# A score scale with its minimum in one VectorE operation, and inverse roots by Newton steps, in a two-layer hybrid attention step

## The chip, the cores and the metric

The kernel runs on one core of one Trainium2 chip. The metric is the time of one execution on the device in microseconds (us), as the median of several runs. The engines are TensorE (PE, its weight loads PEld), VectorE (DVE), ScalarE (ACT), GpSimd (POOL) and SyncE (SP), which here issues nearly all transfers.

## The reference, cut to what matters

Two layers run over 512 latent tokens (four tiles of 128 rows) and 128 context tokens (one tile, here called the prompt). Each layer norms its input, projects it to all branches at once, runs two attentions and a Fourier branch, gates them, projects back and adds to the input. The change touches the softmax of the two attentions and the norms of queries and keys.

```python
def rms_norm(x, g):
    xf = x.astype(jnp.float32)
    y = xf * lax.rsqrt(jnp.mean(xf * xf, axis=-1, keepdims=True) + RMS_EPS)
    return (y * g.astype(jnp.float32)).astype(x.dtype)

def gqa_attention(q, k, v):
    ...
        sc = jnp.einsum('bqhgd,bkhd->bhgqk', qb, k).astype(jnp.float32) * scale
        pr = jax.nn.softmax(sc, axis=-1).astype(v.dtype)
        o = jnp.einsum('bhgqk,bkhd->bqhgd', pr, v)

def diff_attention(q1, q2, k1, k2, v, lam):
    ...
        pr = jax.nn.softmax(s1, axis=-1) - lam * jax.nn.softmax(s2, axis=-1)
        return jnp.einsum('bhqk,bkhd->bqhd', pr.astype(v.dtype), v)
```

Attention A has 8 query heads of 64 on 2 key heads; attention B has 4 heads of two components of 32, so 8 score blocks as well. A latent row sees 512 latent and 256 cached keys, 768 in all; a prompt row sees the 128 prompt keys. `rms_norm` is taken per head: 8 values per row for the queries of A and for queries and keys of B, 2 for the keys of A, over five tiles: 40 or 10 elements per partition.

## The kernel before

**How the program is made.** The functions of `hybrid_step` don't issue instructions; each call records an operation with its inputs, outputs, the engines that may do it and a price per engine (`Engine.cost`, line 451). `Plan.order` (line 187) then simulates the engines with these prices, chooses for each operation the engine and the place in its queue, and for each tile its buffer, and the result is issued in that order. The engines run their queues strictly in it; semaphores do the rest. So a price, a due time (an operation's number plus a shift from the table `SHIFT`) or a constant of `CFG` changes the order of the whole program. `dag`, `dg`, `da` stand for operations that several engines may do (DVE/ACT/POOL, DVE/POOL, DVE/ACT); `dv`, `ac`, `gp`, `pe`, `sp` name one.

**The stages of a layer.** The projections of the five tiles, each in three fp32r products of a high and a low part (whi, wlo from `load_chunk`), come first, with the Fourier branch between them. Then follows attention B, woven with the projections of A, then attention A, woven with the output projection (ohi, olo from `load_wout`, products with mA, mB, mC).

**Queries and keys.** `squares` sums the squares of a head into a tile MS; when all five tiles are there, `rstds` takes the inverse roots with `rstd_of` (line 597): an addition of 1e-6, then one POOL power with exponent -0.5, into a tile rs. Then the rows are scaled by it, staged as fp16 (st), transposed by a transfer (kTB, qTB, kTA, qTA), and scores can begin.

**One unit of attention** (`unit`, line 1217) is one score block of 128 queries by 768 keys; on the prompt it is four heads of 128 by 128. It runs through these steps:

- PE: the score products into a tile S in two PSUM banks (called banks in the profile); at most three S find room.
- DVE: the row maximum m, a reduction over S.
- ACT or DVE: the bias nb = m times minus the scale plus 13 ln 2 (line 1232), on one element per row (four on the prompt).
- ACT: the exponential in place in PSUM, with that bias and the scale KS as operands, and its row sum into Z. So S holds the exponentials times 2 to the 13.
- ACT (or DVE): the cast of S to fp16, the high half of the tile phl.
- DVE: S less that cast, the low half of phl. Then S is free.
- SP: one transposing transfer of phl to pT.
- PE (`unit_back`, line 1246): 18 small products of pT with V, the split values.

The buffers phl (PHL) and pT (PT) are three each. `normed` later multiplies by VI, the value scale from `split_v` (line 996), over Z.

```python
red(m, S.rearrange("p (i k) -> p i k", i=n), ALU.max)
nb = SM([P, n], "nb")
(da if CFG["nb"] else dv).affine(nb, m, KS[a][:, 2:3], shift13)
```

In the profile, line 427 is the call that issues most operations; lines 434, 437, 440 and 443 are the forms of `affine` and `tensor_copy` on ACT, DVE, POOL and ACT. So the tiles tell the operations apart, not the lines.

Of the kernel before, what the change touches and what calls it, by code (L numbers as in the profile page):

```python
# [31 lines left out]
NH = 8  # L32
EPS = 1e-6
GRID_W = 64
LN_SHIFT = 13.0 * math.log(2.0)

C_QA, C_KA, C_VA, C_GA = 0, 512, 640, 768
C_QB, C_KB, C_VB, C_GB, C_UC, C_GC = 1280, 1536, 1792, 2048, 2304, 2560
# [367 lines left out]
class Engine:  # L406
# [43 lines left out]
    @staticmethod  # L450
    def cost(name, op, outs, ins, k, psum):
        o = outs[0]
        n = max([_free(o)] + [_free(x) for x in ins[:1]])
        if op == "dma_start":
            return (450.0 if name == "SP" else 1000.0), max(90.0, _free(o) * o.ap[0][1] * 4 / 360.0)
        if op == "dma_start_transpose":
            return Plan.TURN, _free(o) * 1.0
        if name == "PE":
            m = _free(o)
            if op == "transpose":  # L460
                return 109.0, 0.0
            dt = k["rhs"].dtype
            if dt == F32:
                return (27.0 if o.offset // Plan.row(o) else max(m / 0.6, 213.0)), 0.0
            return (m / 2.4 + 2.4 if dt == F16 else max(m * 0.457 + 1.0, 107.0)), 0.0
        if name == "ACT":
            return ((70.0 if psum else 93.0) + 0.833 * n + 93.0 * (len(ins) - 1)
                    + (112.0 if k.get("accum_out") is not None else 0.0)), 0.0
        if name == "POOL":
            if k.get("op") == ALU.pow:  # L470
                return 200.0 + 60.0 * n, 0.0
            if op == "tensor_tensor":
                still = any(x.ap[-1][0] == 0 for x in ins)
                return 148.0 + (1.67 if still else 1.95 if F16 in (o.dtype, ins[0].dtype) else 2.19) * n, 0.0
            if op == "memset":
                return 100.0 + 0.5 * n, 0.0
            return 161.0 + (0.833 if k.get("op1") is not None or op in ("tensor_copy", "affine") else 3.4) * n, 0.0
        if op == "reciprocal":
            return 65.0 + 8.3 * n, 0.0
        aps = 2 if op == "affine" else sum(isinstance(k.get(q), bass.AP) for q in ("scalar1", "scalar2", "scalar"))  # L480
        fast = op in ("tensor_copy", "tensor_scalar", "affine") and not psum
        return max(130.0, (98.0 if psum and op != "tensor_reduce" else 68.0) + 60.0 * aps + (0.52 if fast else 1.04) * n), 0.0

# [2 lines left out]
def hybrid_step(ctx: ExitStack, tc: tile.TileContext, x_prompt, x_sample, cache_a, cache_b, c, c_ctx,  # L486
# [60 lines left out]
    def ts(eng, out, a, s1, op0, s2=None, op1=None):  # L547
        if op1 is None:
            return eng.tensor_scalar(out=out, in0=a, scalar1=s1, scalar2=None, op0=op0)
        return eng.tensor_scalar(out=out, in0=a, scalar1=s1, scalar2=s2, op0=op0, op1=op1)  # L550
# [29 lines left out]
    pe.transpose(cols_ps, rows, ident[:32, :32])  # L580
    cols = const.tile([P, 32], F32, name="cols")
    dv.tensor_copy(cols, cols_ps)
    shift13 = const.tile([P, 1], F32, name="shift13")
    gp.memset(shift13, LN_SHIFT)
    mhalf = const.tile([P, 1], F32, name="mhalf")
    gp.memset(mhalf, -0.5)
    zero = const.tile([P, 384], F16, name="zero")
# [8 lines left out]

    def rstd_of(out, ms):

        ts(dg, out, ms, EPS, ALU.add)
        y = mk(mhalf, 0, [[0, d[1]] for d in out.ap[1:]])  # L600
        tt(gp, out, out, y, ALU.pow)
# [192 lines left out]
    for l in range(DEPTH):  # L794
# [200 lines left out]
        @moved("scale")  # L995
        def split_v(a):


            n, h0 = (2, 0) if a else (4, 2)
            mx = SM([P, 3], "vm")  # L1000
            parts = []
            for x, i0, m in kv("v", a):
                parts += [(x, 0, min(m, NKEY - i0), i0)] + ([(x, m - 1, m, i0)] if i0 + m > NKEY else [])
            for j, (x, a0, a1, _) in enumerate(parts):
                dv.tensor_reduce(out=mx[:, j:j + 1], in_=x[:, a0:a1], op=ALU.max, axis=AX.XY, apply_absolute_value=True)
            j0 = len(parts) - 2
# [209 lines left out]
        @moved("front")  # L1216
        def unit(a, t, h, z, o):

            n = 4 if t == PT_ else 1
            w = 4 * P if t == PT_ else NKEY * P  # L1220
            nk = w // P
            S = psS([P, w])
            with plan.together():
                if n == 1:
                    qk(S, a, t, h, 0, w)
                else:
                    for i in range(4):
                        qk(S[:, i * P:(i + 1) * P], a, t, h + i, NKEY * P, (NKEY + 1) * P)
            m = SM([P, n], "m")
            red(m, S.rearrange("p (i k) -> p i k", i=n), ALU.max)  # L1230
            nb = SM([P, n], "nb")
            (da if CFG["nb"] else dv).affine(nb, m, KS[a][:, 2:3], shift13)
            k = w // n
            for i in range(n):
                ac.activation(S[:, i * k:(i + 1) * k], S[:, i * k:(i + 1) * k], AF.Exp,
                              bias=nb[:, i:i + 1], scale=KS[a][:, 1:2],
                              accum_out=z[:, i:i + 1])
            hl = alloc(pool, [P, 2, w], F16, "PHL", "phl")
            da.tensor_copy(hl[:, 0, :], S)
            tt(dv, hl[:, 1, :], S, hl[:, 0, :], ALU.subtract)  # L1240
            pt = alloc(pool, [P, 2 * nk, P], F16, "PT", "pT")
            sp.dma_start_transpose(out=pt, in_=hl.rearrange("p a k -> p (a k)"))
            unit_back(a, t, h, n, nk, pt, o)
# [257 lines left out]
 'late': 0.0,  # L1501
 'keep': {'bank': 0, 'G': 2},
 'ahead': 800,
 'late_dma': 0.0,
 'late_pe': 500.0,
 'dve': 1.8,
 'wait': 300.0,
 'start': ['x0', 'm0', 'x3', 'UC', 'x1', 'x2', 'm2', 'm1', 'm3', 'GC', 'x4', 'm4', 'm5', 'm6', 'm7'],
 'fine': 1,
 'nb': 1,  # L1510
 'tail': 3,
 'early': 3,
 'whole': 0,
# [2 lines left out]
 'spare': [],  # L1516
 'early_0': 1,
 'early_1': 2,
 'tail_1': 3}
SHIFT = {'mix': -100, 'fm': -60, 'norm': 10, 'cached': -25, 'mod': -25, 'out': 25, 'qA': 25, 'finish': 250, 'fo': -25, 'cached0': 10, 'finish1': 100, 'start': -25, 'back0': -100}  # L1520
BUFS = {"G": 16, "H": 14, "T": 5, "T2": 2, "W": 8, "KT": 8, "raw": 2, "P": 3, "PHL": 3, "PT": 3, "ST": 2, "O": 2, "Z": 3,
        "KS": 3, "MS": 5, "gmax": 4, "VS": 3, "sm": 11, "gains": 1}

# [78 lines left out]
```

## Time and profile before

| | us |
|---|---|
| median of 3 runs (810.5 to 819.9) | 812.66 |
| the profiled execution | 810.99 |
| its span from first to last instruction | 808.9 |
| PE busy / idle in the span | 708.9 / 100.0 |
| DVE busy | 546.5 |
| ACT busy | 479.2 |
| POOL busy | 297.2 |

The mean clock granted to TensorE is 0.971 of full speed. The page gives busy shares over the whole span, while the stages have different limits; the windows of the trace show them apart. Projections fill about 40 to 180 us (layer 0) and 440 to 560 us (layer 1); attention and output fill 180 to 440 and 560 to 800 us. A line of a group reads: source line, engine, operation, output tile and inputs, shapes and count, then busy us, mean ns of one, and the idle time ahead with what ended it. Matmul records overlap, so their sum exceeds the engine's busy time. The DMA share is the mean busy share of the 16 transfer engines and can exceed 1 where records overlap.

### The profile page before, as it was taken

The numbers are of one execution on the slowest core, as the hardware profiler recorded it, in microseconds if no ns is written. First come the engines' busy times: TensorE is split into PE (matmuls) and PEld (weight loads), VectorE is DVE, ScalarE is ACT, GpSimd is POOL, SyncE is SP. The second block draws the span as 40 slices with busy tenths as digits, with TensorE's granted clock in tenths as the row PEclk, the third lists the DMA queues.
The fourth block names the chain that finished last, engine by engine and source line by source line (L and its number), as shares of the span: only waits on it lengthen the run. The fifth ranks groups of instructions, "written<-read, shape, count | busy, mean of one in ns | idle before, by whom it ended". The sixth has DMA issues, their size and how long they took to land.

```text
span 808.9 us, 17514 instructions
## 1 busy us (share of the span) xinstructions
PE 708.9 (88%) x6752; PEld 583.9 (72%) x6752; DVE 546.5 (68%) x1062; ACT 479.2 (59%) x969; POOL 297.2 (37%) x308
## 2 busy tenths in 40 slices
PE   4899998999988878878879999988978987988886
PEld 2578897888877855545567999988878876656564
DVE  1564264679799659677686432577998866899674
ACT  4763232478768776565786432246875777688651
POOL 2222005435754425272343101444564343624210
PEclk9999999999999979999989999999999998999899
DMA  8967353898999987999996643298899899799884
GB/s 290 338 196 235 98 171 88 211 179 178 195 160 236 251 182 167 227 258 249 258 173 155 214 132 97 67 171 190 169 184 209 179 218 229 125 167 183 140 162 114
DMA packets 316915, 150.50 MB, mean 186 GB/s; under 512 B 256992, under 2 KB 308048, under 8 KB 316832
## 3 DMA queue, kind: packets, MB, share of 16 engines
q1 hardware_dynamic: 314944, 144.21, 79.8%
q0 software_dynamic: 1888, 5.18, 2.2%
q8 instruction: 53, 0.87, 0.5%
q14 instruction: 30, 0.25, 0.1%
HBM read 77.50 MB, written 8.67 MB: 107 GB/s over the span
## 4 chain that ended last, share of the span: by engine, by line
PE 41%; DMA 31%; DVE 9%; POOL 8%; ACT 5%; issue 4%; SPq 1%; ACTq 0%; DVEq 0%; POOLq 0%
PE banks L427 41%; DMA pT_PT<-phl_PHL 18%; POOL rs_MS L427 5%; DMA raw_raw<-in_w_mod_dram 4%; DMA kTB_KT<-st_ST 3%; DVE phl_PHL L427 3%; DVE m_sm L427 2%; DMA rawo_raw<-in_w_out_dram 2%; DMA raw_raw<-in_w_in_dram 2%; ACT phl_PHL L443 2%; ACT banks L427 1%; SPq L427 1%; DMA x_G<-in_x_sample_dram 1%; POOL qA_H L427 1%; POOL wlo_W L427 1%
## 5 line engine op out<-in xcount | busy, mean ns | idle before, releaser
L427 PE MATMUL banks<-whi_W,hhi_G 128*128 128x256 f32 x880 | 252.4, 290 | 7.3 <-ACT sq_T L427 2.7
L427 PE MATMUL banks<-wlo_W,hhi_G 128*128 128x256 f32 x880 | 252.9, 288 | 0.0
L427 PE MATMUL banks<-whi_W,hlo_G 128*128 128x256 f32 x880 | 252.2, 288 | 0.0
L427 PEld LDWEIGHTS banks<-whi_W,hhi_G 128*128 128x128 f32 x880 | 166.5, 190 | 17.3 <-issue 9.5
L427 PEld LDWEIGHTS banks<-wlo_W,hhi_G 128*128 128x128 f32 x880 | 167.3, 190 | 8.7 <-issue 6.6
L427 PEld LDWEIGHTS banks<-whi_W,hlo_G 128*128 128x128 f32 x880 | 167.2, 190 | 5.4 <-issue 3.3
L427 DVE TENSOR_TENSOR phl_PHL<-banks,phl_PHL 128x768 f16<-128x768 f32 (+1 forms) x136 | 126.1, 935 | 33.6 <-ACT phl_PHL L443 33.0
L427 ACT ACTIVATE banks<-banks,nb_sm,KS_KS 128x768 f32<-128x768 f32 (+1 forms) x160 | 136.8, 855 | 2.5 <-DVE mod L427 0.2
L427 DVE TENSOR_REDUCE m_sm<-banks 128x1 f32<-128x768 f32 (+1 forms) x136 | 125.7, 935 | 18.5 <-PE banks L427 15.6
L427 PE MATMUL banks<-V,pT_PT 128*128 128x64 f16 x2400 | 96.5, 196 | 41.8 <-DMA pT_PT<-phl_PHL 37.9
L427 PEld LDWEIGHTS <-pT_PT 128*128 128x128 f16 x2400 | 82.6, 100 | 68.3 <-DMA pT_PT<-phl_PHL 59.1
L443 ACT ACTIVATE phl_PHL<-banks 128x768 f16<-128x768 f32 (+1 forms) x135 | 106.2, 797 | 34.5 <-DMA pT_PT<-phl_PHL 33.2
L434 ACT ACTIVATE nb_sm<-m_sm,shift,KS_KS 128x1 f32<-128x1 f32 (+1 forms) x106 | 40.4, 383 | 67.0 <-DVE m_sm L427 56.7
L427 PE MATMUL banks<-ohi_W,mA_G 128*128 128x512 f32 x160 | 58.7, 426 | 4.7 <-ACT ohi_W L443 3.2
L427 PE MATMUL banks<-kTA_KT,qTA_H 128*128 128x512 f16 (+2 forms) x288 | 56.9, 332 | 3.7 <-DVE phl_PHL L427 3.4
L427 POOL TENSOR_TENSOR xo_G<-xo_G,go_T 128x512 f32<-128x512 f32 x24 | 31.6, 1320 | 73.1 <-DVE go_T L427 72.9
L427 DVE TENSOR_TENSOR wlo_W<-raw_raw,whi_W 128x1024 fp32r<-128x1024 f32 x33 | 40.3, 1224 | 15.7 <-ACT whi_W L443 8.9
L443 ACT ACTIVATE whi_W<-raw_raw 128x1024 fp32r<-128x1024 f32 x34 | 36.1, 1060 | 19.3 <-DMA raw_raw<-in_w_in_dram 17.3
L427 PEld LDWEIGHTS <-qTA_H 128*128 128x128 f16 x288 | 25.4, 105 | 30.0 <-issue 14.0
L427 POOL TENSOR_TENSOR rs_MS<-rs_MS,mhalf 128x40 f32<-128x40 f32 (+1 forms) x8 | 44.6, 5581 | 0.4
L427 PEld LDWEIGHTS banks<-ohi_W,mA_G 128*128 128x128 f32 x160 | 30.6, 196 | 13.7 <-ACT ohi_W L443 3.9
L427 ACT ACTIVATE sq_T<-banks 128x256 f32<-128x256 f32 (+1 forms) x50 | 17.9, 359 | 37.7 <-PE banks L427 31.6
(257 smaller groups left out, 1147.1 us busy)
## 6 DMA issues: line engine op xcount, KB each, us to landing
raw_raw<-in_w_in_dram SPq DMA_DIRECT2D x44, 512.0 KB, 5.0
raw_raw<-in_w_mod_dram SPq DMA_DIRECT2D x32, 512.0 KB, 4.4
rawo_raw<-in_w_out_dram SPq DMA_DIRECT2D x16, 512.0 KB, 5.1
x<-xo_G SPq DMA_DIRECT2D x10, 512.0 KB, 4.7
xo_G<-x SPq DMA_DIRECT2D x10, 512.0 KB, 5.3
dft_G<-in_dft_s_dram POOLq DMA_DIRECT2D x8, 512.0 KB, 4.3
raw_P<-in_w_mod_dram SPq DMA_DIRECT2D x11, 256.0 KB, 5.5
raw_PHL<-in_w_mod_dram SPq DMA_DIRECT2D x11, 256.0 KB, 5.2
```

The source lines that it names most:

```text
L427: return getattr(real, op)(*[at(x) for x in a], **{q: at(v) for q, v in k.items()})
L434: ways.append((name, dur, dma, lambda real=real: real.activation(at(outs[0]), at(a[1]), AF.Identity, bias=at(a[3]), scale=at(a[2])), None, ...
L443: ways.append((name, dur, dma, lambda real=real: real.activation(at(outs[0]), at(ins[0]), AF.Copy), None, port))
```

## The change

- For a unit of 768 keys, one DVE operation multiplies S in PSUM by minus the scale, writes it back in place, and gives the row minimum as its accumulator m. ACT's exponential takes m as bias with the constant factor -1. The reduction over S and the step nb are gone. On the prompt the reduction stays; a small DVE product gives the bias.
- The factor 2 to the 13 moves from the bias to the cast (now an `affine` with that factor) and to the difference (`scalar_tensor_tensor`); `split_v` divides VI by it.
- `rstd_of` on more than 8 elements (the queries and keys of A and B, eight times in the kernel) is an integer start value and three Newton steps on DVE, eleven instructions in two scratch tiles. Smaller ones keep the POOL power.
- The planner's price of the POOL power rises, its price of a DVE operation counts an accumulator and fewer operands for `affine`, and constants of `CFG` and `SHIFT` are set anew.

```diff
-                return 200.0 + 60.0 * n, 0.0
+                return 440.0 + 158.0 * n, 0.0
...
     def rstd_of(out, ms):
 
+        if _free(out) > 8:
+            v, a = (alloc(pool, [P] + list(out.shape[1:]), F32, "rstd", "r") for _ in range(2))
+            ts(dv, v, ms, EPS, ALU.add)
+            ts(dv, out.bitcast(I32), v.bitcast(I32), -0.5, ALU.mult, 1597463007.0, ALU.add)
+            for _ in range(3):
+                tt(dv, a, out, out, ALU.mult)
+                stt(a, a, -0.5, v, ALU.mult, ALU.mult)
+                stt(out, a, 1.5, out, ALU.add, ALU.mult)
+            return
         ts(dg, out, ms, EPS, ALU.add)
...
             dv.reciprocal(vs, vi)
+            ts(dv, vi, vi, 2.0 ** -13, ALU.mult)
...
             m = SM([P, n], "m")
-            red(m, S.rearrange("p (i k) -> p i k", i=n), ALU.max)
-            nb = SM([P, n], "nb")
-            (da if CFG["nb"] else dv).affine(nb, m, KS[a][:, 2:3], shift13)
             k = w // n
-            for i in range(n):
-                ac.activation(S[:, i * k:(i + 1) * k], S[:, i * k:(i + 1) * k], AF.Exp,
-                              bias=nb[:, i:i + 1], scale=KS[a][:, 1:2],
-                              accum_out=z[:, i:i + 1])
+            if n == 1:
+                dv.tensor_scalar(out=S, in0=S, scalar1=KS[a][:, 2:3], scalar2=3e38, op0=ALU.mult, op1=ALU.min, accum_out=m)
+                ac.activation(S, S, AF.Exp, bias=m, scale=-1.0, accum_out=z)
+            else:
+                red(m, S.rearrange("p (i k) -> p i k", i=n), ALU.max)
+                ts(dv, m, m, KS[a][:, 2:3], ALU.mult)
+                for i in range(n):
+                    ac.activation(S[:, i * k:(i + 1) * k], S[:, i * k:(i + 1) * k], AF.Exp,
+                                  bias=m[:, i:i + 1], scale=KS[a][:, 1:2], accum_out=z[:, i:i + 1])
             hl = alloc(pool, [P, 2, w], F16, "PHL", "phl")
-            da.tensor_copy(hl[:, 0, :], S)
-            tt(dv, hl[:, 1, :], S, hl[:, 0, :], ALU.subtract)
+            da.affine(hl[:, 0, :], S, 2.0 ** 13, 0.0)
+            stt(hl[:, 1, :], S, 2.0 ** 13, hl[:, 0, :], ALU.mult, ALU.subtract)
...
- 'late_dma': 0.0,
- 'late_pe': 500.0,
- 'dve': 1.8,
- 'wait': 300.0,
+ 'late_dma': 500.0,
+ 'late_pe': 650.0,
+ 'dve': 1.9,
+ 'wait': 250.0,
...
- 'tail_1': 3}
+ 'tail_1': 2}
...
+ 'kA1': -170,
+ 'norm1': 50,
```

What the order does with it shows at three places. The first is ACT at the end of attention A in layer 1, before; Z is the row sum, KS the scale, mA the gated output of a tile.

```order
L434 ACTIVATE nb_1931_sm_12274<-m_1930_sm_12267,shift_79,KS_1342_KS_8071 128x1
L427 ACTIVATE mA_1946_G_12278<-banks 128x256
L427 ACTIVATE banks,Z_1883_Z_11999<-banks,nb_1931_sm_12274,KS_1342_KS_8071 128x768
L443 ACTIVATE phl_1932_PHL_12290<-banks 128x768
L434 ACTIVATE nb_1940_sm_12338<-m_1939_sm_12330,shift_79,KS_1342_KS_8071 128x1
```

The same place now:

```order
L433 ACTIVATE phl_1796_PHL_11894<-banks 128x768
L426 ACTIVATE banks,Z_1768_Z_11757<-banks,m_1801_sm_11915 128x768
L433 ACTIVATE phl_1802_PHL_11930<-banks 128x768
L426 ACTIVATE banks,Z_1768_Z_11757<-banks,m_1805_sm_11928 128x768
L433 ACTIVATE phl_1806_PHL_11959<-banks 128x768
```

The nb rows are gone, the exponential reads m itself, and KS is no longer among its operands.

The second place is the inverse root of the keys of B in layer 0. On POOL before (ko is the prompt's keys on their way out, kB the keys):

```order
L427 TENSOR_SCALAR rs_349_MS_3345<-MS_330_MS_3202 128x40
L427 TENSOR_TENSOR rs_349_MS_3345<-rs_349_MS_3345,mhalf 128x40
L427 TENSOR_TENSOR ko_350_T_3398<-kB_275_G_2615,rs_349_MS_3345 128x256
L427 TENSOR_TENSOR kB_274_G_3258<-kB_274_G_3258,rs_349_MS_3345 128x1024
L440 TENSOR_SCALAR st_369_ST_3431<-kB_274_G_3258 128x4x96
```

On DVE now, where r are the scratch tiles and mod the modulation of the next layer:

```order
L426 TENSOR_SCALAR r_349_rstd_3227<-MS_329_MS_3067 128x40
L426 TENSOR_TENSOR t_262_347_T_3230<-banks,tabB_210_H_2543 128x256
L426 TENSOR_SCALAR rs_348_MS_3237<-r_349_rstd_3227 128x40
L426 TENSOR_TENSOR kB_273_G_3137<-kB_273_G_3137,t_262_347_T_3230 128x256
L426 TENSOR_TENSOR r_350_rstd_3242<-rs_348_MS_3237 128x40
L426 SCALAR_TENSOR_TENSOR r_350_rstd_3242<-r_350_rstd_3242,r_349_rstd_3227 128x40
L426 SCALAR_TENSOR_TENSOR rs_348_MS_3237<-r_350_rstd_3242,rs_348_MS_3237 128x40
```

The addition and the power left POOL; the chain stands on DVE among the last evacuations of the keys, two more rounds of three behind the rows shown.

The third place is the end of PE's queue. Before, from the last product with pT (V are the values) on:

```order
L427 MATMUL banks<-V,pT_1942_PT_12378 128x64
L427 MATMUL banks<-olo_1849_W_11797,mA_1946_G_12278 128x512
L427 MATMUL banks<-ohi_1848_W_11766,mA_1946_G_12278 128x512
L427 MATMUL banks<-ident,gA_1599_H_10472 128x128 x2
L427 MATMUL banks<-ohi_1851_W_11871,mA_1946_G_12278 128x512
```

Now:

```order
L426 MATMUL banks<-V,pT_1817_PT_12024 128x64
L426 MATMUL banks<-ohi_1743_W_11494,mA_1819_G_11861 128x512
L426 MATMUL banks<-olo_1744_W_11532,mA_1819_G_11861 128x512
L426 MATMUL banks<-ohi_1743_W_11494,mA_1819_G_11861 128x512
L426 MATMUL banks<-ohi_1746_W_11545,mA_1819_G_11861 128x512
L426 MATMUL banks<-olo_1747_W_11557,mA_1819_G_11861 128x512
L426 MATMUL banks<-ohi_1746_W_11545,mA_1819_G_11861 128x512
L426 MATMUL banks<-ohi_1749_W_11644,mA_1819_G_11861 128x512
L426 MATMUL banks<-olo_1750_W_11657,mA_1819_G_11861 128x512
L426 MATMUL banks<-ohi_1749_W_11644,mA_1819_G_11861 128x512
L426 MATMUL banks<-ident,gA_1519_H_10231 128x128 x2
```

Between the last product with pT and the transposes of the gated rows gA, which wait for it by way of DVE, stood two output products, and now nine of another tile.

More of the change, by code (lines that the diff above doesn't have):

```diff
@@ L34 @@
 GRID_W = 64
-LN_SHIFT = 13.0 * math.log(2.0)
 C_QA, C_KA, C_VA, C_GA = 0, 512, 640, 768
@@ L479, in cost @@
             return 65.0 + 8.3 * n, 0.0
-        aps = 2 if op == "affine" else sum(isinstance(k.get(q), bass.AP) for q in ("scalar1", "scalar2", "scalar"))
+        aps = len(ins) - 1 if op == "affine" else (k.get("accum_out") is not None) + sum(isinstance(k.get(q), bass.AP) for q in ("scalar1", "scalar2", "scalar"))
         fast = op in ("tensor_copy", "tensor_scalar", "affine") and not psum
@@ L582, in hybrid_step @@
     dv.tensor_copy(cols, cols_ps)
-    shift13 = const.tile([P, 1], F32, name="shift13")
-    gp.memset(shift13, LN_SHIFT)
     mhalf = const.tile([P, 1], F32, name="mhalf")
@@ L1503 @@
  'ahead': 800,
- 'late_dma': 0.0,
- 'late_pe': 500.0,
- 'dve': 1.8,
- 'wait': 300.0,
+ 'late_dma': 500.0,
+ 'late_pe': 650.0,
+ 'dve': 1.9,
+ 'wait': 250.0,
  'start': ['x0', 'm0', 'x3', 'UC', 'x1', 'x2', 'm2', 'm1', 'm3', 'GC', 'x4', 'm4', 'm5', 'm6', 'm7'],
  'fine': 1,
- 'nb': 1,
  'tail': 3,
@@ L1518 @@
  'early_1': 2,
- 'tail_1': 3}
-SHIFT = {'mix': -100, 'fm': -60, 'norm': 10, 'cached': -25, 'mod': -25, 'out': 25, 'qA': 25, 'finish': 250, 'fo': -25, 'cached0': 10, 'finish1': 100, 'start': -25, 'back0': -100}
+ 'tail_1': 2}
+SHIFT = {'mix': -100,
+ 'fm': -60,
+ 'norm': 10,
+ 'cached': -25,
+ 'mod': -25,
+ 'out': 25,
+ 'qA': 15,
+ 'finish': 250,
+ 'fo': -25,
+ 'cached0': 10,
+ 'finish1': 100,
+ 'start': -25,
+ 'back0': -100,
+ 'kA1': -170,
+ 'norm1': 50,
+ 'norm0': -10,
+ 'start0': -45,
+ 'back1': -160,
+ 'rows0': 40,
+ 'fab0': -160}
 BUFS = {"G": 16, "H": 14, "T": 5, "T2": 2, "W": 8, "KT": 8, "raw": 2, "P": 3, "PHL": 3, "PT": 3, "ST": 2, "O": 2, "Z": 3,
-        "KS": 3, "MS": 5, "gmax": 4, "VS": 3, "sm": 11, "gains": 1}
+        "KS": 3, "MS": 5, "rstd": 4, "gmax": 4, "VS": 3, "sm": 11, "gains": 1}
 def _split12(x):
```

## The prediction, as it was recorded

> **What bounds the kernel now.** I read the page first: busy shares, then the chain that ended last; then the windows, which put a stage to each share; then the waits of TensorE.
>
> ```profile
> span 808.9 us, 17514 instructions
> PE 708.9 (88%) x6752; PEld 583.9 (72%) x6752; DVE 546.5 (68%) x1062; ACT 479.2 (59%) x969; POOL 297.2 (37%) x308
> PE 41%; DMA 31%; DVE 9%; POOL 8%; ACT 5%; issue 4%; SPq 1%; ACTq 0%; DVEq 0%; POOLq 0%
> PE banks L427 41%; DMA pT_PT<-phl_PHL 18%; POOL rs_MS L427 5%; DMA raw_raw<-in_w_mod_dram 4%; DMA kTB_KT<-st_ST 3%; DVE phl_PHL L427 3%; DVE m_sm L427 2%; DMA rawo_raw<-in_w_out_dram 2%; DMA raw_raw<-in_w_in_dram 2%; ACT phl_PHL L443 2%; AC
> ```
>
> TensorE (PE) is the busiest engine, but the chain spends 31% on transfers, most of it on pT, the transposed probabilities. The reduction m_sm, the POOL power rs_MS and the difference phl_PHL, which the change touches, are on the chain with 2, 5 and 3%.
>
> ```profile
> 120.00:180.00 60.00, 53.72 (x426) 47.98 (x426) 36.74 (x88) 25.16 (x59) 26.48 (x17) 0.94 0.70 160
> 180.00:440.00 260.00, 221.32 (x2317) 174.44 (x2316) 199.14 (x337) 183.31 (x357) 118.66 (x122) 0.96 0.97 206
> 520.00:560.00 40.00, 35.97 (x291) 33.99 (x290) 25.39 (x64) 18.40 (x39) 21.47 (x13) 0.96 0.73 155
> 560.00:800.00 240.00, 208.77 (x2224) 167.08 (x2222) 193.19 (x307) 167.57 (x333) 96.96 (x88) 0.97 0.92 178
> PE banks L427 <- DMA pT_PT<-phl_PHL: 37.9, 38, 2.4
> PE banks L427 <- DVE phl_PHL L427: 10.8, 15, 1.8
> ```
>
> Columns: window, length, PE, PEld, DVE, ACT, POOL, granted clock, DMA share, GB/s. The second and fourth rows are the attention stages of the two layers; the first and third are the ends of the projections ahead of them. In attention PE idles 38.7 and 31.2 us, VectorE (DVE) is busy 77 and 80%, and the DMA engines stand at 0.97 and 0.92: no engine is full but the transfers nearly are. PE's two largest waits are there: 38 times for a transposed block, 15 times for a score bank that the difference has not freed. Ahead of attention PE idles 6.3 and 4.0 us.
>
> **Part 1, the path of one unit (128 units of 768 keys, 8 of the prompt).** The last unit of the kernel, which nothing queues in front of, shows it:
>
> ```profile
> 788.83 0.96 DVE L427 TENSOR_REDUCE m_sm<-banks 128x1 f32<-128x768 f32 x1
> 789.82 0.39 ACT L434 ACTIVATE nb_sm<-m_sm,shift,KS_KS 128x1 f32<-128x1 f32 x1 [4.09 <-DVE m_sm L427]
> 790.24 0.96 ACT L427 ACTIVATE banks<-banks,nb_sm,KS_KS 128x768 f32<-128x768 f32 x1
> 798.28 0.70 PE L427 MATMUL banks<-V,pT_PT 128*128 128x64 f16 x18 [0.95 <-DMA pT_PT<-phl_PHL]
> ```
>
> From the maximum's start to its products takes 9.5 us. The bias step nb_sm costs 0.45 (789.79 to 790.24); a hand-over alone costs 0.03 (789.79 to 789.82). So its removal gives 0.42.
>
> ```profile
> L427 DVE TENSOR_REDUCE m_sm<-banks 128x1 f32<-128x768 f32 x128 | 120.3, 950 | 15.4 <-PE banks L427 12.5 <-ACT phl_PHL L443 1.1 <-POOL rb_sm L427 0.8
> L427 DVE TENSOR_TENSOR phl_PHL<-banks,phl_PHL 128x768 f16<-128x768 f32 x128 | 120.7, 951 | 32.7 <-ACT phl_PHL L443 32.1
> L427 DVE SCALAR_TENSOR_TENSOR V<-vA_G,vs_sm,V 128x768 f16<-128x768 f32 x2 | 2.0, 1008 | 0.0
> L427 ACT ACTIVATION_READ_ACCUMULATOR banks<-banks,nb_sm,KS_KS 128x1 f32 x160 | 31.5, 197 | 0.0
> L427 ACT ACTIVATE banks<-banks,nb_sm,KS_KS 128x768 f32<-128x768 f32 x128 | 123.1, 961 | 2.3 <-DVE mod L427 0.2
> L443 ACT ACTIVATE phl_PHL<-banks 128x768 f16<-128x768 f32 x127 | 101.7, 809 | 33.7 <-DMA pT_PT<-phl_PHL 32.5
> L434 ACT ACTIVATE nb_sm<-m_sm,shift,KS_KS 128x1 f32<-128x1 f32 x98 | 37.3, 383 | 58.8 <-DVE m_sm L427 48.5 <-POOL ob_T L427 7.0 <-POOL xo_G L427 3.1
> L437 DVE TENSOR_SCALAR nb_sm<-m_sm,KS_KS,shift 128x1 f32<-128x1 f32 x30 | 7.9, 267 | 1.1 <-ACT nb_sm L434 0.4
> ```
>
> The scale with minimum takes the reduction's place. No row shows DVE writing PSUM or giving an accumulator. A pass over 768 with a per-partition scalar costs 1.008 (the V row; 0.057 above the difference), which is the low bound; if the minimum has to be read out like ScalarE's sum (the accumulator row, 0.197), 1.205. I take 1.10, between them. VectorE: DVE Perf Modes (the Trainium skill, "Two Vector instructions with no wait between them") says that an op which also writes out its accumulator is two instructions, the main one and an accumulator read; the trace shows such a pair on ACT alone, and by that rule the upper bound holds and the unit's gain below is 0.24. The exponential loses one of two per-partition operands: 961 less 809 (a pass with none) is 152, half of it 0.076. Cast and difference gain a constant factor: nothing for the cast (bounds 0 and +0.076), nothing for the difference (bounds 0 and +0.057). The prompt's eight units keep the reduction and add a 4-element scale of about 0.2 in place of an nb of 0.39: nothing.
>
> Sum per unit: -0.42 + 0.15 - 0.08 = -0.35 (bounds -0.44 and -0.24). ACT loses 37.3 + 3.1 us of nb and 128 x 0.076 = 9.7, which matters little: ACT is 70% busy in attention. DVE gains 128 x 0.15 = 19 and loses 7.9.
>
> What reaches the end is set by PE's 53 waits, 48.7 us. Each shrinks by at most 0.35: 18.6 us. The new order helps too: counted in 256-column matmuls, the weight products that stand on PE between a unit's scores and its pT products rise from 52.6 to 57.0 on average, and in the least covered tenth of the units from 24 to 38. Where nothing but such products run, 175 of them fill 20 us:
>
> ```profile
> 480.00:500.00 20.00, 20.00 (x175) 20.00 (x173) 4.96 (x9) 5.06 (x14) 1.05 (x1) 1.00 0.33 104
> ```
>
> That is 0.114 each, so 0.5 us more cover per unit. Together 0.85 us against a mean wait of 0.92 would take nearly all 48.7. But a transfer can't come sooner than the queue allows:
>
> ```profile
> pT_PT<-phl_PHL SPq DMA_TRANSPOSE x136, 4.2
> DMA to landing us min/median/max: 3.0/4.2/8.5
> 772.94 8.53 SPq L427 DMA_TRANSPOSE pT_PT<-phl_PHL  x4
> ```
>
> The median landing is 1.2 above the least, and four in a row leave the queue 2.1 us apart. The DMA share leaves 3% of 260 and 8% of 240: 7.8 + 19.2 = 27 us, the ceiling. The floor is 0 (transfers take it all back). I take 11, two fifths, since at 0.97 and 0.92 the row that it is nearest to is a full queue.
>
> **Part 2, the norms' inverse roots.**
>
> ```profile
> L427 POOL TENSOR_TENSOR rs_MS<-rs_MS,mhalf 128x40 f32<-128x40 f32 x6 | 40.7, 6780 | 0.2
> L427 POOL TENSOR_TENSOR rs_MS<-rs_MS,mhalf 128x10 f32<-128x10 f32 x2 | 4.0, 1982 | 0.2
> L427 POOL TENSOR_SCALAR rs_MS<-MS_MS 128x40 f32<-128x40 f32 x6 | 2.0, 328 | 39.6 <-DVE MS_MS L427 39.5
> L427 DVE TENSOR_SCALAR rs_MS<-rs_MS,gmax_gmax 128x40 f32<-128x40 f32 x2 | 0.5, 244 | 7.9 <-POOL rs_MS L427 7.9
> L427 DVE TENSOR_TENSOR mod<-mod,bcols 128x4 f32<-128x4 f32 x16 | 2.5, 159 | 0.4
> ```
>
> Eight POOL pairs (7.1 us for 40 elements, 2.3 for 10) become eight chains of 11 DVE instructions: two scalings and three rounds of three. One costs between 0.159 (4 elements) and 0.244 (40 elements with a pointer operand); I take 0.20, so 2.2 us a chain: 4.9 sooner for keys and queries of B in each layer, ahead of attention. DVE takes on about 8 x 2.1 = 17 us, POOL loses 46. But PE is 90% busy while the power runs, and the first scores stand no earlier among PE's rows than before, so all that can be had is PE's idle time there, 6.3 + 4.0 = 10.3; the other end is 3 lost, if the chains stand in front of PSUM evacuations. I take 5, half.
>
> Against this speaks a port row:
>
> ```profile
> L427 DVE TENSOR_TENSOR qA_H<-qA_H,rs_MS 128x512 f32<-128x512 f32 x1 | 1.6, 1583 | 0.0
> L427 DVE TENSOR_TENSOR qB_H<-qB_H,rs_MS 128x512 f32<-128x512 f32 x2 | 1.4, 692 | 5.4 <-POOL rs_MS L427 5.4
> ```
>
> The same DVE operation took 0.89 longer while POOL worked. Nine of a chain's 11 instructions have two SBUF inputs. In the first window POOL is busy 26.5 us, 12.9 without its two powers: 15 operations of 0.86, 21% of the time. If each of the nine met half an operation in 21% of cases, a chain would last 9 x 0.21 x 0.43 = 0.8 longer: 4.1 left of 4.9. SBUF — State Buffer (the Trainium skill, "SBUF: two separate sides") calls this an exclusive lock, held for the whole instruction by whichever starts first; the 1583 agrees, and by that rule the term would be 4 where I have 5.
>
> The chains of queries and keys of A (2.2 + 1.8, both layers: 8 us) lie in attention, where DVE is 77 to 80% busy: a quarter of it delays a unit, +2.
>
> **Part 3, the re-set order.** Beside the cover counted above, weight differences move from DVE (33 to 25) to POOL (11 to 19):
>
> ```profile
> L427 DVE TENSOR_TENSOR wlo_W<-raw_raw,whi_W 128x1024 fp32r<-128x1024 f32 x33 | 40.3, 1224 | 15.7 <-ACT whi_W L443 8.9 <-POOL whi_W L440 5.8 <-PE banks L427 0.8
> L427 POOL TENSOR_TENSOR wlo_W<-raw_raw,whi_W 128x1024 fp32r<-128x1024 f32 x11 | 27.0, 2453 | 14.1 <-ACT whi_W L443 13.8
> ```
>
> That gives DVE 9.8 us back and POOL 19.6 of the 46 it lost. Each is 1.23 later; chunks are loaded ahead of their use and the list of PE's waits names no wlo, so nothing (1.23 each, 9.8 in all, if that cover is gone). At the end, nine output products instead of two follow the last pT product and cover its evacuation; PE waits there now:
>
> ```profile
> 800.02 0.44 PE L427 MATMUL banks<-ident,gA_H 128*128 128x128 f32 x2 [0.49 <-DVE gA_H L427]
> 800.93 0.50 PE L427 MATMUL banks<-ohi_W,mA_G 128*128 128x512 f32 x1 [0.47 <-ACT mA_G L427]
> ```
>
> With the 0.95 ahead of the last pT that is 1.9; I take 1. Nothing else moved has a price that I can read.
>
> **The sum** against the profiled execution (810.99, of it 808.9 span): -11 - 5 + 2 - 1 = -15, so 796. That execution is 1.7 below the median of the runs, 812.66.
>
> **The rivals.**
> 1. Transfers hide it: pT queues as before, the -11 is 0 and the rest nets a few us: 805 to 812. For it: 0.97 and the 18% of pT in the chain. Against: 0.92 in layer 1, and 38 waits that average only 1 us.
> 2. The order settles nearly all PE waits: -27 - 10 - 2 = 772, so 771 to 786. For it: 0.85 us against 0.92. Against: the full queue.
> 3. Slower: reading and writing PSUM in one DVE instruction takes two passes. The scale costs about 2.0 us, DVE gains 64 x 1.05 = 67 us a layer and loses 7 to nb and wlo: 199 + 60 and 193 + 60. Of its idle time, 61 and 47, a fifth stays: 271 and 262 us for stages of 260 and 240, so 811 + 33 - 8 = 836, or 820 with half of that. It decides from some 0.7 us extra per unit (45 us a layer leaves DVE some 8% idle). Against it: the exponential reads and writes the same bank and pays only its operands.
> 4. The locks of the port eat the Newton gain and slow the chains in attention: the -5 becomes 0 and the +2 becomes 5: 804 to 810.
>
> That the change doesn't do what it says is excluded by the order: the nb steps and the eight wide powers are gone from it.
>
> **How the numbers follow.** My case (787 to 804) 0.48, rival 2 0.17, rival 1 0.19, rival 4 0.05, rival 3 0.11. The time is that of the likeliest, 796. The range 778 to 816 leaves out rival 3 and the deeper half of rival 2, 0.19. Under 1% nothing can be told apart here; faster by more (below 804.5) 0.65, within 1% 0.24, slower 0.11.
>
> **What would show it.** In the new profile: the scale row of 768 at 1.0 to 1.2 (2.0 is rival 3); rs_MS off the chain; DVE at 560 to 575 us, ACT near 430, POOL near 270; PE's waits for pT at some 25 us instead of 37.9, and for phl no more than 10.8 (37.9 unchanged with a DMA share near 1 is rival 1; under 10 is rival 2). I am wrong if PE's waits move to another name, above all to wlo from POOL or to banks held by DVE.

## The result and the profile after

The changed kernel takes 785.62 us (median of 4 runs, 784.35 to 790.51), the kernel before 811.62 (4 runs): a ratio of 0.966, with a 95% interval of 0.960 to 0.973. The forecast was 796, in a range of 778 to 816. The direction and the range hold; the gain is 26 us where 15 was forecast, and the experiments show that most of it does not come from where the sum had it. The profiled execution took 786.54 (before: 810.99). One execution of the run e6 below took 1325 us; its ratio leaves it out, and the median of the other three is 781.34.

The page of the kernel after: span, busy times, and the chain that ended last by engine and by line.

```profile
span 784.8 us, 17483 instructions
PE 699.3 (89%) x6752; PEld 577.4 (74%) x6752; DVE 555.6 (71%) x1230; ACT 439.1 (56%) x874; POOL 272.6 (35%) x310
PE 50%; DMA 30%; DVE 9%; ACT 4%; issue 3%; POOL 2%; SPq 1%; ACTq 0%; DVEq 0%; POOLq 0%
```

ACT and POOL lost the work that the sum took from them (479 to 439, 297 to 273), DVE gained 9, POOL fell from 8% of the chain to 2%, and transfers stayed at 30%. Now the windows of the kernel after, at the same times as before (columns as in the prediction; the fourth, 560 to 800, reaches past the end of this kernel):

```profile
120.00:180.00 60.00, 57.26 (x492) 52.24 (x491) 45.67 (x122) 26.50 (x56) 26.08 (x26) 1.00 0.75 175
180.00:440.00 260.00, 226.62 (x2353) 178.03 (x2353) 204.55 (x397) 169.44 (x329) 106.08 (x119) 0.97 1.02 214
520.00:560.00 40.00, 36.92 (x315) 35.58 (x314) 34.21 (x77) 24.87 (x57) 20.41 (x21) 1.00 0.84 172
```

PE idles less ahead of attention (2.7 us of the 60, before 6.3) and in the attention of layer 0. The waits of PE:

```profile
PE banks L426 <- DMA pT_PT<-phl_PHL: 24.9, 32, 1.8
PE banks L426 <- DVE phl_PHL L426: 10.7, 20, 1.4
PE banks L426 <- ACT gA_H L442: 4.5, 5, 1.5
PE banks L426 <- DVE O_O L426: 3.8, 5, 1.8
```

The waits for pT fell from 37.9 to 24.9, those for phl stayed (10.8 and 10.7). The rows of the changed unit, of the power that became a chain, and of the moved differences:

```profile
L426 DVE TENSOR_SCALAR_CACHE_REDUCE banks<-banks,KS_KS 128x768 f32<-128x768 f32 x128 | 128.0, 1020 | 19.1 <-PE banks L426 18.4
L426 DVE DVE_READ_ACCUMULATOR banks<-banks,KS_KS 128x1 f32 x128 | 18.0, 141 | 0.0
L426 ACT ACTIVATE banks<-banks,m_sm 128x768 f32<-128x768 f32 x128 | 111.9, 875 | 62.3 <-DVE banks L426 56.3
L426 DVE SCALAR_TENSOR_TENSOR rs_MS<-r_rstd,rs_MS 128x40 f32<-128x40 f32 (+1 forms) x24 | 4.5, 189 | 0.3
L426 POOL TENSOR_TENSOR wlo_W<-raw_raw,whi_W 128x1024 fp32r<-128x1024 f32 x19 | 45.6, 2406 | 5.7 <-ACT whi_W L442 5.5
```

The sizes of the single instructions came out as forecast: the scale with minimum is one pass and a read-out, and the eleven steps of a chain are busy for about 2 us. So the surprise has to lie between the instructions. The lengths of the stages, read from the timelines of PE (first pT product to last pT product of a layer; one execution each, in us):

| kernel (median of its runs) | to the first pT product | attention, layer 0 | between | attention, layer 1 | behind |
|---|---|---|---|---|---|
| before (811.6) | 183.5 | 248.7 | 137.6 | 228.5 | 10.6 |
| after (785.6) | 178.8 | 244.7 | 133.1 | 214.7 | 13.5 |
| e2, Newton in the old order (811.2) | 176.8 | 254.2 | 134.1 | 231.6 | 10.6 |
| e4, old constants (808.0) | 175.0 | 249.3 | 134.6 | 231.6 | 10.5 |
| e5, look-ahead 810 (796.1) | 177.3 | 255.6 | 137.2 | 217.6 | 13.2 |
| e6, old wait price (783.0) | 180.0 | 237.6 | 134.4 | 214.9 | 10.8 |
| e7, old shifts (788.9) | 180.1 | 238.8 | 141.1 | 218.1 | 13.5 |
| e8, bias step put back (786.8) | 177.8 | 240.6 | 133.7 | 217.2 | 13.4 |
| e9, cover alone (805.0) | 175.5 | 248.4 | 137.8 | 238.1 | 10.5 |
| e10, powers put back (800.2) | 186.3 | 243.8 | 138.6 | 213.9 | 13.8 |

Of 24.1 us of span, 4.7 and 4.5 come ahead of the two attention stages, 4.0 in that of layer 0, 13.8 in that of layer 1; 2.9 are given back at the end. A stage of one order differs by some 4 us from run to run (after and e8, whose order is the same), so single differences near that are weak. The profiled execution of e4 is its fastest (802.92), those of e5 and e9 are their slowest (802.68 and 812.13).

### The profile page after: what moved, and what is told of

Same layout as the page of the kernel before. It is cut to its first block, busy times and chain, and to the rows that moved or that the text cites. A ratio compares the mean times of both kernels' runs of the same rounds, so it can differ in the third digit from the quotient of the medians.

```text
span 784.8 us, 17483 instructions
## 1 busy us (share of the span) xinstructions
PE 699.3 (89%) x6752; PEld 577.4 (74%) x6752; DVE 555.6 (71%) x1230; ACT 439.1 (56%) x874; POOL 272.6 (35%) x310
## 4 chain that ended last, share of the span: by engine, by line
PE 50%; DMA 30%; DVE 9%; ACT 4%; issue 3%; POOL 2%; SPq 1%; ACTq 0%; DVEq 0%; POOLq 0%
PE banks L426 50%; DMA pT_PT<-phl_PHL 20%; DMA kTB_KT<-st_ST 3%; DMA rawo_raw<-in_w_out_dram 3%; DVE phl_PHL L426 3%; ACT phl_PHL L433 2%; DVE banks L426 1%; SPq L426 1%; ACT banks L426 1%; DMA raw_PT<-in_w_mod_dram 1%; DMA raw_raw<-in_w_mod_dram 1%; DMA qTB_H<-st_ST 1%; DMA rows_T<-in_norm_g_dram 1%; DMA raw_raw<-in_w_in_dram 1%; DVE go_T L426 1%
## 5 line engine op out<-in xcount | busy, mean ns | idle before, releaser
L426 DVE SCALAR_TENSOR_TENSOR phl_PHL<-banks,phl_PHL 128x768 f16<-128x768 f32 (+1 forms) x136 | 125.9, 937 | 38.8 <-ACT phl_PHL L433 38.2
L426 ACT ACTIVATE banks<-banks,m_sm 128x768 f32<-128x768 f32 x128 | 111.9, 875 | 62.3 <-DVE banks L426 56.3
L426 DVE TENSOR_SCALAR_CACHE_REDUCE banks<-banks,KS_KS 128x768 f32<-128x768 f32 x128 | 128.0, 1020 | 19.1 <-PE banks L426 18.4
L426 PE MATMUL banks<-V,pT_PT 128*128 128x64 f16 x2400 | 94.1, 195 | 30.3 <-DMA pT_PT<-phl_PHL 24.9
L426 PEld LDWEIGHTS <-pT_PT 128*128 128x128 f16 x2400 | 80.3, 99 | 54.6 <-DMA pT_PT<-phl_PHL 39.3
L426 POOL TENSOR_TENSOR xo_G<-xo_G,go_T 128x512 f32<-128x512 f32 x23 | 29.4, 1281 | 73.1 <-DVE go_T L426 73.0
L426 POOL TENSOR_TENSOR wlo_W<-raw_raw,whi_W 128x1024 fp32r<-128x1024 f32 x19 | 45.6, 2406 | 5.7 <-ACT whi_W L442 5.5
L426 DVE TENSOR_TENSOR wlo_W<-raw_raw,whi_W 128x1024 fp32r<-128x1024 f32 x25 | 31.7, 1269 | 14.7 <-ACT whi_W L442 12.9
L426 PE MATMUL banks<-kTB_KT,qTB_H 96*128 96x256 f16 (+2 forms) x144 | 33.4, 322 | 7.3 <-DVE phl_PHL L426 4.2
L426 PE MATMUL banks<-ohi_W,mB_H 128*128 128x512 f32 x80 | 32.8, 445 | 5.2 <-DVE mB_H L426 3.4
```

The source lines that it names most:

```text
L426: return getattr(real, op)(*[at(x) for x in a], **{q: at(v) for q, v in k.items()})
```

## The experiments

The theories. A: the instructions gained, the shorter path of a unit above all, as the sum has it. B: the order gained; in its form K, because more PE work stands between scores and pT products. L: the re-set constants are right as such. M: something else in the order gained. C: the transfers cap what can be had. The runs came in three groups, each beside runs of the kernel before on the same chip (medians 811.1 for e1 to e4, 813.3 for e5 to e8, 812.7 for e9 to e12); ratios are to these, with 95% intervals.

**Instructions and order taken apart.** In before the list of operations is planned as it was, and only what an operation issues is exchanged, by a function that replaces the issuing part of the operation recorded last. The front:

```diff
             red(m, S.rearrange("p (i k) -> p i k", i=n), ALU.max)
+            if n == 1:
+                plan.swap(lambda e, f: nc.vector.tensor_scalar(out=ap_(S), in0=ap_(S), scalar1=ap_(ks), scalar2=3e38,
+                                                               op0=ALU.mult, op1=ALU.min, accum_out=lo))
...
             (da if CFG["nb"] else dv).affine(nb, m, KS[a][:, 2:3], shift13)
+            if n == 1:
+                plan.swap(lambda e, f: None)
```

with the new exponential, cast, difference and factor of VI exchanged in the same way (ap_ gives the place of a tile, lo and ks are the unit's minimum and its factor).

> The order of before on every engine, with the new unit front issued in it: the scale with minimum at the reduction's place, nothing at the bias step's place, the new exponential, cast and difference at theirs. Theory A (the shorter front is what gained; the order only follows): each of the 53 PE waits shrinks by up to 0.35 us, so 12 to 19 us faster than before (793 to 800). Theory B (the re-set order gained most, because it puts more matmuls between scores and pT products): no more than 6 us (805 to 812). Theory C (the queue of pT transfers is full): 0 to 3 us, and the PE waits for pT stay near 38 us.

Measured: 805.18, ratio 0.993 (0.990 to 0.996), 5.5 us faster. This is theory B's number, and less than half of the least that A expected. PE's waits for pT hardly moved (35.7 us in 37). Where the path's gain went shows on ACT, in the row of the cast, before and in this run:

```profile
L443 ACT ACTIVATE phl_PHL<-banks 128x768 f16<-128x768 f32 (+1 forms) x135 | 106.2, 797 | 34.5 <-DMA pT_PT<-phl_PHL 33.2
```

```profile
L1254 ACT ACTIVATE phl_PHL<-banks 128x768 f16<-128x768 f32 (+1 forms) x135 | 106.3, 797 | 44.3 <-DMA pT_PT<-phl_PHL 42.5
```

The cast waits 9 us longer for a phl buffer that an earlier transpose still reads: part of what the front gains it waits for the transfers.

The Newton chains alone, at the places of addition and power:

```diff
+        plan.swap(lambda e, f: ve.tensor_scalar(out=v, in0=at(ms), scalar1=EPS, scalar2=None, op0=ALU.add))
         y = mk(mhalf, 0, [[0, d[1]] for d in out.ap[1:]])
         tt(gp, out, out, y, ALU.pow)
+        plan.swap(chain)
```

where chain issues the other ten steps on DVE, for outputs of more than 8 elements.

> The order of before, with the eight wide powers replaced by Newton chains on DVE at the same places; the unit front as before. My term: 4.9 us sooner ahead of attention in each layer, half of PE's idle time there, minus 2 in attention: 3 us faster (806 to 809). Rival (the order, set for late powers, does not use the earlier roots, or the port locks eat them): within 1.5 us of before. Rival (the power stood on the path at its full length): 8 to 12 us faster.

Measured: 811.24, ratio 1.000 (0.997 to 1.004). The rival holds. The table says how: attention begins 6.7 us sooner in layer 0, and the stretch between the stages is 3.5 shorter, but the attention stages are 5.5 and 3.1 longer, so that their ends stand within 2 us of where they stood. The last three of these differences are near the scatter of the table; that the 6.7 us sooner start brings nothing at the end is shown by the medians.

> The order of before with both changes issued in it. What separates it from the changed kernel is the order alone. Theory A (instructions): 788 to 793, within 5 us of the changed kernel. Theory B (order): 800 to 809, so that 15 us or more of the 26 are the order's. If the two parts simply add, the gain is the sum of the two runs above.

Measured: 808.33, ratio 0.996 (0.993 to 0.999), 3 us of the 26. All instructions of the change, in the order of before, are worth no more than that: theory A falls for that order.

The next run leaves the changed kernel as it is, its prices too, and takes back only the planner's constants and shifts:

```diff
- 'late_dma': 500.0, 'late_pe': 650.0, 'dve': 1.9, 'wait': 250.0, ... 'tail_1': 2
+ 'late_dma': 0.0, 'late_pe': 500.0, 'dve': 1.8, 'wait': 300.0, ... 'tail_1': 3
```

(and the shifts of before.)

> The changed kernel's instructions and prices, planned with the constants and shifts of before (no re-setting). Theory A: 786 to 792. Theory B in its narrow form (the re-set constants gained): 797 to 808. If the planner given the new prices finds a good order by itself, this run is near the changed kernel while the one above is not.

Measured: 807.97, ratio 0.996 (0.992 to 0.999), as theory B's narrow form had it. The same instructions, planned anew with the old constants, are as slow as in the old order. The re-set constants and shifts carry about 22 us by the medians. The two profiled executions lie 16 apart, and the attention of layer 1 alone differs by 17 in them.

**What in the order it is.** Three re-plannings of the changed kernel, with ahead 810, wait 300, and the old shifts:

> The changed kernel with one constant moved that no part of the change speaks of (how many operations the planner may look ahead, 810 instead of 800), so that it draws another order. In that order 24 weight products stand between scores and pT products in the least covered tenth of the units, as in the order of before (24) and in that of the old constants (23), where the changed kernel has 38. Theory K (that cover is what gained): 803 to 810, with PE's waits for pT at 40 us or more. Theory L (the new constants are right as such, the waits' prices above all, which stay): 784 to 791.

> The changed kernel with one of its own re-set constants put back (wait 300 instead of 250). Its order differs, but its least covered tenth has 35 weight products, nearly the changed kernel's 38. Theory K (cover): 784 to 791. Theory L (each re-set constant bears its share): 790 to 800.

> The changed kernel with the re-set constants and the old shifts. The least covered tenth of its order has 38 products in layer 0, as the changed kernel, but 20 in layer 1, where the changed kernel has 38 too. Theory K (cover): layer 0 lasts as long as in the changed kernel, layer 1 as long as with the old constants (15 us more in the stretch from first to last pT product): 796 to 804. Theory L: the shifts only set the tail and the starts, 786 to 792.

Measured: e5 796.14, ratio 0.980 (0.975 to 0.986); e6 782.96, ratio 0.963 (0.958 to 0.968); e7 788.90, ratio 0.971 (0.966 to 0.976). In e5 a constant that has no bearing on the change costs 10 us, so one draw of the planner can differ from another by about as much. That is neither K's 803 to 810 nor L's 784 to 791, and the waits for pT are 35.3 us, not 40. The second run is a little faster than K expected and well outside L. The third lies within L's 786 to 792 and is against K: its layer 1 lasts 218.1, with 20 products in the least covered tenth, nearly as short as in the changed kernel with 38, and 13 shorter than e4.

Cover alone, with all else in e4's order in its place:

```diff
+            while have < COVER and at + 1 < len(out) and not clash(b, out[at + 1][1][0]):
+                at += 1
+                if out[at][1][1] == "PE":
+                    have += out[at][1][2]
+            out.insert(at, out.pop(q))
```

Here b is a unit's block of pT products, have the PE work between its scores and them, and clash says that the next row needs the block or takes a buffer from it.

> The order of the run with the old constants (808 us), of which one thing is changed: where less than 9.5 us of TensorE work by the planner's prices stands between a unit's scores and its pT products, these products are put behind the next rows until 9.5 are reached or something needs them. Summed over the units, what is missing to 9.5 falls from 111 us to 49 (35 in the changed kernel); all else keeps its place. Theory K (cover is what the new order gained): the gain follows what is missing, 22 us for 76, so 18 us for 62: 786 to 796. Theory M (it is something else in the order, such as which work stands outside attention or on which engine): 803 to 812, the waits only move to a later row.

Measured: 805.01, ratio 0.991 (0.987 to 0.995), where e4 has 0.996 (0.992 to 0.999): some 4 us, with the two intervals anything from nothing to 8, and not the 18 that K expected. The cover itself was reached: counted in PE's busy time in the traces, what is missing to 9.5 us falls from 45 us in e4 to 5, and it is 6 in the changed kernel. Theory K falls. PE's waits for pT and for banks held by DVE in e4, then in this run:

```profile
PE banks L426 <- DMA pT_PT<-phl_PHL: 44.3, 42, 3.4
PE banks L426 <- DVE phl_PHL L426: 6.2, 8, 2.3
```

```profile
PE banks L448 <- DMA pT_PT<-phl_PHL: 22.0, 25, 2.7
PE banks L448 <- DVE phl_PHL L448: 15.1, 16, 2.4
PE banks L448 <- DVE t_T L448: 9.5, 4, 3.3
```

The waits for pT are halved, and the time hardly moves: 9 us of them stand now at score banks that DVE has not freed, and as much at banks of the projections that wait for DVE's t (0.4 in e4). So PE's wait for pT was a place at which lateness showed, not its cause. The two lists come from executions that lie 9 us apart, so their sums are no balance.

The same later placing in the changed kernel and in e6:

> The changed kernel with the same later placing of pT products: what is missing to 9.5 us of cover falls from 35 us to 11. Theory K at its rate of 0.29 us for each us of cover: 7 us faster than the changed kernel, 776 to 782. Theory C (from here on the transfers and their buffers set the pace): 783 to 788.

> The run with the old wait price (783 us) with the same later placing: what is missing falls from 36 us to 10. Theory K: 7 us faster than that run, 773 to 779. Theory C: 780 to 785.

Measured: 785.32, ratio 0.967 (0.964 to 0.970), no change; and 790.87, ratio 0.972 (0.970 to 0.974), 8 us slower than e6, though its waits for pT fell from 26.2 to 18.8. Theory C's number for the first, nobody's for the second.

**The instructions in the new order.** One edit puts a one-element step back between minimum and exponential:

```diff
                 ac.activation(S, S, AF.Exp, bias=m, scale=-1.0, accum_out=z)
+                plan.swap(lambda e, f: (plan.pin(nc.scalar.activation(nb, at(m), AF.Identity, bias=zz, scale=one)),
+                                        nc.scalar.activation(at(S), at(S), AF.Exp, bias=nb, scale=-1.0, accum_out=at(z)))[1])
```

> The changed kernel's order, with a one-element ScalarE step put back between the scale with minimum and each of the 128 exponentials (it copies the bias). If the shorter front counts in this order as my sum had it, 128 units with some 45 waits lose up to 0.42 us each: 6 to 15 us slower than the changed kernel (792 to 801). If the longer cover hides the step, within 3 us of it (784 to 789).

Measured: 786.80, ratio 0.968 (0.964 to 0.971). In the new order the step costs nothing that can be told. ACT's waits for a phl buffer, in the changed kernel and with the step:

```profile
ACT phl_PHL L433 <- DMA pT_PT<-phl_PHL: 48.2, 46, 3.4
```

```profile
ACT phl_PHL L437 <- DMA pT_PT<-phl_PHL: 13.9, 14, 2.9
```

ACT is busy 44 us longer with the steps and waits 34 us less. The step takes 0.383 us, as much as the whole path of a unit had gained (0.38, below). The shorter front mostly came sooner to a buffer that was not free.

The other edit puts the eight wide inverse roots back on POOL, and issues nothing at nine steps of each chain.

> The changed kernel's order with the eight wide inverse roots back on POOL (one addition and one power at the place of the chain's first two steps, nothing at the other nine). By my term, with the roots 5 us later ahead of attention in a plan that counts on them: 4 to 10 us slower than the changed kernel (790 to 796). If the work that stands there covers it, as in the old order, within 2 us (784 to 788).

Measured: 800.21, ratio 0.984 (0.981 to 0.987), 14 us slower than the changed kernel, more than either side expected. By the table it is all ahead of attention (+7.5 and +5.5), the attention stages are as long as in the changed kernel. The reverse edit is worth nothing in the old order (e2). The rows of POOL in this run, at the keys of B in layer 0:

```profile
125.33 0.33 POOL L605 TENSOR_SCALAR r_rstd<-MS_MS 128x40 f32<-128x40 f32 x1 [4.36 <-DVE MS_MS L430]
125.75 6.79 POOL L607 TENSOR_TENSOR rs_MS<-r_rstd,mhalf 128x40 f32<-128x40 f32 x1
132.99 0.62 POOL L430 TENSOR_TENSOR ko_T<-kB_G,rs_MS 128x256 f32<-128x256 f32 x1 [0.45 <-DVE rs_MS L430]
```

and the same place in the changed kernel, first and last step of the chain and what follows:

```profile
125.68 0.17 DVE L426 TENSOR_SCALAR r_rstd<-MS_MS 128x40 f32<-128x40 f32 x1
...
128.97 0.20 DVE L426 SCALAR_TENSOR_TENSOR rs_MS<-r_rstd,rs_MS 128x40 f32<-128x40 f32 x1
```

The root is done at 129.17 instead of 132.54, with other evacuations between the chain's steps. These 3.4 us are not yet the 7.5. More comes with the next power, that of the queries of B; rows of POOL, DVE and PE in e10 (row_T is a row of the modulation that PE transposes):

```profile
150.92 6.78 POOL L607 TENSOR_TENSOR rs_MS<-r_rstd,mhalf 128x40 f32<-128x40 f32 x1
157.68 0.43 POOL L443 TENSOR_SCALAR st_ST<-kB_G 128x288 f16<-128x288 f32 x1
158.15 2.14 DVE L430 TENSOR_TENSOR st_ST<-kB_G,st_ST 128x96 f16<-128x96 f32 x2 [7.50 <-POOL st_ST L443]
161.94 0.69 PE L430 MATMUL banks<-ident,row_T 128*128 128x128 f32 x2 [4.64 <-ACT row_T L446]
```

Behind the power in POOL's queue stands a staging step of the keys, which ran at 149.92 in the changed kernel. DVE idles 7.5 us for it, ACT 6.5 us for queries that DVE scales after that, and PE 4.6 us for row_T, which stands behind these in ACT's queue. So a late root held up work that doesn't use it, because the plan had put that work behind the root.

**Read together.** The split of the 26 us depends on what is exchanged first. In the old order the instructions bring 3 us and the new order the other 23. From the other end, the new order with the powers on POOL is 12 to 13 us faster than before, and the early roots bring the other 14. So some 10 us of the gain come only with both. e10 may overstate the roots, since it puts powers at places that were laid out for chains.

**The granted clock as a rival.** The profiled executions have 0.957 to 0.991, and in some kernels the execution with the higher clock is the faster one (e9: 801.21 at 0.984, 810.43 at 0.968). It does not make the differences named here. At 0.971 the changed kernel took 784.35 and the kernel before 810.99; e4 took 802.92 and e10 798.13 at 0.975; e5 took 792.26 at 0.970, so 8 of its 10 us are left at an equal clock.

## Why the prediction was right and wrong, step by step

**The path of a unit: right.** The scale starts at 759.62 and its minimum is out at 760.70, 1.08 us where 1.10 was taken:

```profile
759.62 1.03 DVE L426 TENSOR_SCALAR_CACHE_REDUCE banks<-banks,KS_KS 128x768 f32<-128x768 f32 x1 [0.57 <-PE banks L426]
760.56 0.14 DVE L426 DVE_READ_ACCUMULATOR banks<-banks,KS_KS 128x1 f32 x1
```

The exponential lost 0.086 (0.08 was taken), cast and difference changed by no more than 3 ns (809 to 812, 951 to 952). So the path of a unit is 0.38 us shorter, 0.35 by the forecast. That an instruction with an accumulator is two, as VectorE: DVE Perf Modes (the Trainium skill, "Two Vector instructions with no wait between them") has it, agrees with these rows; the second begins before the first ends, so the price by the sum of both, 1.16, is 0.08 too high. Rival 3, two passes for PSUM, is out at 1.02 (its "some 8% idle" holds for layer 0 alone; by the same sum layer 1 would have 4%).

**From the path to the end: wrong.** "What reaches the end is set by PE's 53 waits" is the step that failed, and with it the -11. PE's waits for pT are no budget: e9 halves them for some 4 us, and e8 has them at 10.7 against 24.9 in the same time, while its waits for banks grew by 6.6:

```profile
PE banks L430 <- DVE phl_PHL L430: 17.3, 26, 3.9
PE banks L430 <- DMA pT_PT<-phl_PHL: 10.7, 18, 1.2
```

The front as such gains 5.5 us in the old order, and in the new one the step that it saved costs nothing measurable when it is put back. Rival 1's mechanism, a queue that takes the gain back, is what e1 and e8 show on ACT, though its time did not come, because the order gained elsewhere.

That the time lies in the range, and that nearly all the signs came (waits for pT of 24.9 where 25 was said, for phl 10.7 where no more than 10.8 was), is luck in this part: most of the gain hangs on the order, of which the sum had only the cover, and the cover is not what gained. Even PE's idle time fell by nearly the 15 of the sum (100.0 to 85.5 us), and the other 9.6 us of the span are PE's busy time for the same 6752 instructions. But e8 reaches the same time with 76.4 idle and 706.3 busy, so neither part is a budget.

**The cover, 0.5 us a unit: wrong.** The count is right, the new order does put more products there, but e9, e11 and e12 show that it is not what gained. The new order is what the result hangs on: both sets of instructions bring 3 us in the old order and 26 in the new. Rival 2's time (771 to 786) came, and not by its mechanism, since PE still waits 36 us for pT and phl.

**The ceiling of 27 us from the DMA share: wrong as a measure.** The rows of the attention of layer 1, before, after and in e8:

```profile
569.80:798.30 228.50, 198.76 (x2133) 158.13 (x2132) 182.81 (x286) 160.09 (x311) 91.85 (x83) 0.97 0.93 179
```

```profile
556.60:771.30 214.70, 189.88 (x2099) 150.81 (x2097) 178.37 (x347) 141.05 (x272) 85.89 (x82) 0.98 0.98 188
```

```profile
552.10:769.30 217.20, 194.37 (x2099) 154.53 (x2097) 178.45 (x347) 163.00 (x333) 85.64 (x81) 0.97 0.90 186
```

The share went up with the speed, and in e8 it is 0.90 at nearly the speed at which the changed kernel shows 0.98. The changed kernel stayed below the ceiling in both layers (4.0 of 7.8, 13.8 of 19.2), but e6 did not: its attention of layer 0 is 11.1 shorter than before. In layer 0 the share goes above 1:

```profile
178.80:423.50 244.70, 211.32 (x2227) 164.46 (x2227) 193.43 (x382) 158.99 (x310) 103.16 (x115) 0.97 1.05 216
```

**The inverse roots: nearly right in length, wrong in worth.** The steps of a chain are busy 2.1 us, 2.2 were taken. With the steps of others between them a chain spans 3.5, so the first root comes 3.7 us sooner after its squares than with the power, not 4.9. The -5 was held between -10.3, PE's idle time ahead of attention, and +3. It is 0 in the old order and -14 in the new one, with about -13 ahead of attention. The bound failed because the idle time of the old plan says nothing of how a plan stalls that was laid out for early roots; the rows of e10 show such a stall. Of the 13 us, 7.2 are PE's idle time and the rest is busy time for the same PE instructions. The +2 for the chains of A within attention agrees with e10 in sign and size (+0.9 and +0.8), below what one profile each can tell; in the old order the attention stages lost 8.6. Rival 4 is neither seen nor excluded as a mechanism: a step on 40 elements lasts 0.17 to 0.20 on average in the changed kernel, but POOL worked during only 0.6 of the 13.5 us of two-input steps there. In e2 and e4 one step each that met POOL took 0.72 and 0.62. Its time did not come.

**The moved differences, nothing: right** as to waits: 19 stand on POOL, and PE waited 0.8 us for them, in two waits. **The end, -1: right as to waits.** PE waits for nothing there any more (1.9 us before). The stretch is 2.9 us longer all the same, since 20 more PE instructions stand behind the last pT product (PE busy 8.6 us instead of 4.7): work that moved there from elsewhere.

**What stays open** is which property of the order is worth the 22 us between e4 and the changed kernel, and which constants bring it: with the wait price alone put back the time is 783, with the shifts alone 789, and the other four constants were not put back one by one. Layer 1 shows it most: there PE runs 2099 instructions in the stage and DVE is busy 178 us, while in e4, the stage of 231.6 us, it is 2141 and 187:

```profile
558.90:790.50 231.60, 202.13 (x2141) 160.34 (x2139) 186.64 (x357) 144.61 (x273) 89.14 (x80) 0.96 0.88 177
```

Of the 16.9 us by which this stage of e4 is longer, 12.2 are PE's busy time (42 instructions more, at a granted clock of 0.96 instead of 0.98) and 4.7 its idle time, so PE's waits are the smaller part. In all runs with a short stage (up to 221 us) DVE is busy at most 181 us in it, in all with a long one (from 226) at least 182, e9 among these (190). Less work inside attention, on DVE above all, is thus the candidate (theory M); it goes along with the time and was not tested alone, and a longer stage also holds more of an engine's work, so it may be an effect. Nor was the whole old set of instructions run in the new order.

## What to carry to other kernels

Where a planner draws the order, measure the new instructions in the old order, and the new order with the old instructions put back one by one: here the two parts were worth 5.5 and 0 us alone and 3 together in the old order, and 26 in the new one, and a constant of no meaning for the change moved the time by 10. A list of waits names where lateness shows; before a sum is built on it, ask what the waiting engine, and the buffers behind it, would wait for next. A bound taken from idle time in one plan need not hold for another plan: 10.3 us of idle time were there, and 14 were at stake.

## What the runs showed of the hardware that was not expected

The busy share of the DMA engines is no gauge of room: it reached 1.05 over 245 us, and 0.90 and 0.98 at rates of 186 and 188 GB/s. The accumulator's read-out starts 0.09 us before the main instruction's end. A scaling of 768 scores in place in PSUM (1.020 us) costs 0.07 more than the reduction that only reads them. A VectorE step on 40 elements took 0.17 to 0.20 us on average, so eleven of them are a third of GpSimd's one power on 40 (6.78 us). And a lower granted clock did not always go with a longer time: the changed kernel's fastest run (784.35 us) had 0.971, its profiled one (786.54) 0.982, while e9's fastest run (801.21) had 0.984 and its two slowest (810.43 and 812.13) 0.968 and 0.972.
